# Both MLP entries: the residual sum kept in its PSUM bank, and the norm's matmuls placed behind the first two products

## The chip, the cores and the metric

The kernel runs on one core of a Trainium2 chip. The core has five engines with queues of their own: TensorE (PE in the profile, its weight loads PEld), VectorE (DVE), ScalarE (ACT), GpSimd (POOL) and SyncE (SP), which issues the DMAs here. TensorE writes only to PSUM, which has eight banks of 128 partitions x 512 f32 values. The other working memory is SBUF. The metric is the device time of one execution in microseconds; smaller is better.

## The reference

The model has two residual layers over 512 positions of width 1024, each a mixer followed by an MLP, each behind an RMSNorm. What matters here is the seam between mixer and MLP:

```python
for layer in range(DEPTH):                      # DEPTH = 2
    h = _rmsnorm(x, mix_norm_g[layer])
    x = x + mixer(h) @ w_out                    # layer 0: gMLP + stick-breaking attention
                                                # layer 1: mLSTM
    h = _rmsnorm(x, mlp_norm_g[layer])
    x = x + jnp.square(jax.nn.relu(h @ w1)) @ w2    # w1: 1024 x 4096, w2: 4096 x 1024

def _rmsnorm(x, g):
    ms = jnp.mean(xf * xf, axis=-1, keepdims=True)
    return xf * lax.rsqrt(ms + EPS) * g
```

All of it is f32.

## The kernel before, in words

The residual x lies in SBUF transposed, as `xs`: eight pieces d = 0 to 7 of 128 features x 512 positions. To come close to f32 results, every operand of a product is split into two halves of a shorter type: a high half made by ScalarE (`act.activation(..., Copy)`, L189, L282, L286) and a low half, the rest, made by VectorE (L190, L283, L287; for a few weights by GpSimd). A product is then three matmuls (`mm3`, L290 to L292).

**Weights.** They come as a stream of 128 x 1024 blocks. `w_load` (L182) has SP issue the DMA, `w_split` makes the halves, and `w_take` asks for some blocks and has six more prepared ahead. Five pairs of halves fit in SBUF at once, so a block's halves are made when an older pair has been used up.

**The mixer's output product.** `w_out` (L321 to L328) makes the eight pieces of `mixer(h) @ w_out` one after another. Each takes a PSUM bank from a tag (A has 2 banks, B 3, C 2, O 1), runs its matmuls, and VectorE adds bank and residual into `xs` (L327). In layer 0 a piece is 12 matmuls on banks in the order A, A, B, B; in layer 1 the last part is 6 matmuls a piece on A, A, O.

**The entry.** `enter` (L330 to L342) consumes these pieces. For each it makes the halves of x times the norm's gain, `xhi` and `xlo` (L333), and the square of x on ScalarE (L335, L338); GpSimd adds the squares to one sum `ssq` (L339), VectorE the last of them. The squares share one buffer (tag jk), so a square waits until the one before it is added. When all eight are in, `norm_cols` (L261 to L271) sums `ssq` over the features with four matmuls against a column of 1/1024 (L266, eight instructions in the trace) into a bank of tag C, VectorE adds EPS (L268), and GpSimd raises it to the power -1/2 (L270). `norm_row` (L273 to L279) spreads the result to all partitions with four transposes (L277), and ScalarE copies them out of the bank into `rrow` (L278).

The norm's row scale isn't in `xhi` and `xlo`: it is applied behind the first product of the MLP.

**The MLP.** `mlp` (L620 to L740) runs four groups. In a group, eight first products (24 matmuls each: 8 pieces of x, three matmuls a piece) go to banks of tag A and C in turn; VectorE makes `max(b, 0) * rrow` (L733) and ScalarE squares it (L734). The second products follow, in a Strassen-like scheme (L658 to L714) on banks of tags B and O.

**What sets the order.** The program is written as one stream; the framework notes which instruction needs which, and a planner then orders each engine's queue by a model of the instructions' times, the earlier of two ready ones in the program first. Tiles of one tag take their buffers in program order. Each queue on the chip runs strictly in the order that the planner wrote. The framework puts the accesses of different engines to one bank in order.

Of the kernel before, what the change touches and what calls it, by code (L numbers as in the profile page):

```python
# [132 lines left out]
def _program(ctx, tc, nc, I, O):  # L133
    pool = lambda n, b=1: ctx.enter_context(tc.tile_pool(name=n, bufs=b))
    act, dve, pe, gp = nc.scalar, nc.vector, nc.tensor, nc.gpsimd
    f = lambda t: t.bitcast(F32)
# [121 lines left out]
    onesd = const.tile([P, P], F32, name="onesd")  # L258
    gp.memset(onesd, 1.0 / D)

    def norm_cols(ssq):  # L261

        n = len(ssq)
        b = bank("C")
        for t in range(n):
            pe.matmul(b[:, t:t + 1], lhsT=ssq[t], rhs=onesd[:, 0:1], start=True, stop=True)  # L266
        me = sm(n, f"me{n}")
        dve.tensor_scalar(me, b[:, :n], EPS, None, op0=ALU.add)  # L268
        r = sm(n, f"rc{n}")
        gp.tensor_tensor(r, me, nhalf[:, :n], op=ALU.pow)  # L270
        return me, r  # L271

    def norm_row(r, dst):  # L273

        b = bank("B")
        for t in range(NT):
            pe.transpose(b[:, tts(t)], r[:, t:t + 1].to_broadcast([P, P]), ident)  # L277
        act.activation(dst, b, AF.Copy)  # L278
        rb[0] = dst  # L279

    def split_scaled(dhi, dlo, src, g):
        act.activation(dhi, src, AF.Copy, scale=g)  # L282
        dve.scalar_tensor_tensor(dlo, src, g, f(dhi), op0=ALU.mult, op1=ALU.subtract)  # L283
# [5 lines left out]
    def mm3(out, lh, ll, rh, rl, first, last):  # L289
        pe.matmul(out, lhsT=lh, rhs=rh, start=first, stop=False)  # L290
        pe.matmul(out, lhsT=lh, rhs=rl, start=False, stop=False)  # L291
        pe.matmul(out, lhsT=ll, rhs=rh, start=False, stop=last)  # L292

    junk = pool("junk")
    nhalf = const.tile([P, 8], F32, name="nhalf")
# [12 lines left out]
    tags = itertools.cycle("AAO")  # L308
# [9 lines left out]
                    kt == 0, kt == KT - 1)  # L318
            evac(t, b[:, :width])

    def w_out(hus, ys, tags="A"):  # L321

        for d in range(KT):
            b = bank(tags[d % len(tags)])
            for k, (hi, lo) in enumerate(hus):
                mm3(b, hi[:, tts(d)], lo[:, tts(d)], ys[k][0], ys[k][1], k == 0, k == len(hus) - 1)
            dve.tensor_tensor(xs[:, d, :], b, xs[:, d, :], op=ALU.add)  # L327
            yield d  # L328

    def enter(gen, norm, ssq):  # L330

        for i, d in enumerate(gen):
            split_scaled(xhi[:, d, :], xlo[:, d, :], xs[:, d, :], pc(f"g{norm}", d))  # L333
            if i == 0:
                act.activation(ssq, xs[:, d, :], AF.Square)  # L335
            else:
                j = junk.tile([P, T], F32, name=f"sq{norm}_{d}", tag="jk", bufs=1)
                act.activation(j, xs[:, d, :], AF.Square)  # L338
                (dve if i == KT - 1 else gp).tensor_tensor(ssq, ssq, j, op=ALU.add)  # L339
        r = norm_cols([ssq[:, tts(t)] for t in range(NT)])[1]  # L340
        r1[:] = [r[:, t:t + 1] for t in range(NT)]
        return r  # L342


    ev = ExitStack()
# [4 lines left out]
    with ExitStack() as gx:  # L350
# [22 lines left out]
        b = bank("C")  # L373
# [75 lines left out]
    with ExitStack() as ax:  # L449
        ap = ax.enter_context(tc.tile_pool(name="at", bufs=1))  # L450
# [3 lines left out]
        yb = lambda k, n: (vc[:, :, 2 * k - n].rearrange("p t e d -> p t (e d)") if n <= k else  # L454
                           xlo[:, KT - 1, :].rearrange("p (t c) -> p t c", t=NT))
# [144 lines left out]
        fill.clear()  # L600
        for _ in pieces:
            pass
        ssq = ap.tile([P, T], F32, name="ssq0", tag="m3", bufs=1)
        r = enter(w_out(w_take(4), [(yb(k, 0), yb(k, 1)) for k in range(4)], "AABB"), 1, ssq)
    ev.close()
    nrm = pool("nrm")
    ssq = nrm.tile([P, T], F32, name="ssq")
    rrow = nrm.tile([P, T], F32, name="rrow")
    norm_row(r, rrow)

# [6 lines left out]
    PROD = ("a11", "s2", "n3", "a12", "-a22", "n1", "n4")  # L617
    H = T // 2

    def mlp(last, nxt):  # L620
        with tc.tile_pool(name="mlp", bufs=1) as mp:
            qpool[0] = mp
            accm = mp.tile([P, 4, H], F32, name="accm")
# [34 lines left out]
            def second(g, ops):  # L658

                for s in range(2):  # L660
# [48 lines left out]
                    for e, d in enumerate((4 + 2 * s, 5 + 2 * s)):  # L709
                        add(xs[:, d, :H], b[:, e])  # L710
                        if last and done:
                            nc.sync.dma_start(out=O["out"][d][:, :H], in_=xs[:, d, :H])
                        if done:
                            yield d  # L714

            def out(nb, s):
                for d in (4 * nb + 2 * s, 4 * nb + 2 * s + 1):
                    yield d

            for g in range(NG):  # L720
                ops = {n: [mp.tile([P, 4, H], F32R, name=f"{n}{e}_{g}", tag=f"{n}{e}", bufs=1) for e in "hl"] for n in PROD}
                for q in range(2):
                    hr = []
                    for kb in range(2):
                        hr.append(mp.tile([P, 2, T], F32, name=f"h{g}{q}{kb}", tag="h", bufs=3))
                        for e in range(2):
                            (wh, wl), = w_take(1)
                            b = bank("AC"[e])
                            for kt in range(KT):
                                cs = slice(kt * P, (kt + 1) * P)  # L730
                                mm3(b, wh[:, cs], wl[:, cs], xhi[:, kt, :], xlo[:, kt, :], kt == 0, kt == KT - 1)
                            r = mp.tile([P, T], F32, name=f"r{cnt[0]}", tag="r", bufs=2)
                            dve.scalar_tensor_tensor(r, b, 0.0, rb[0], op0=ALU.max, op1=ALU.mult)  # L733
                            act.activation(hr[kb][:, e, :], r, AF.Square)  # L734
                    operands(q, hr, ops)
                if g == NG - 1 and nxt:
                    norm_row(enter(second(g, ops), nxt, ssq), rrow)
                else:
                    for _ in second(g, ops):
                        pass  # L740

    mlp(False, 2)
# [20 lines left out]
    with ExitStack() as ox:  # L763
# [153 lines left out]
        for op, h, n in ODD:  # L917
# [15 lines left out]
    norm_row(r, rrow)  # L933
    vx.close()
    mlp(True, None)


# [9 lines left out]
```

## Time and profile before

| what | value |
|---|---|
| median of the runs | 1131.99 us |
| profiled execution | 1132.91 us |
| its span, first to last instruction | 1131.1 us |
| TensorE busy | 1107.5 us (98%) |
| VectorE busy | 820.4 us (73%) |
| ScalarE busy | 524.6 us (46%) |
| GpSimd busy | 158.4 us (14%) |
| mean granted TensorE clock | 0.994 |

The profile's lines name an operation by source line, engine and tiles: `L283 DVE ... xlo<-xres,par,xhi` is line 283 of the kernel, on VectorE, which reads `xres` (the residual `xs`), `par` (the gains) and `xhi`, and writes `xlo`. Names that begin with `ps` are PSUM banks by tag. In a timeline a row has start, duration, engine, line, operation and count, and in brackets the idle time of the engine ahead of it with what ended it. Matmul rows overlap, since they are pipelined: what counts is the distance between their starts.

### The profile page before, as it was taken

The numbers are of one execution on the slowest core, as the hardware profiler recorded it, in microseconds if no ns is written. First come the engines' busy times: TensorE is split into PE (matmuls) and PEld (weight loads), VectorE is DVE, ScalarE is ACT, GpSimd is POOL, SyncE is SP. The second block draws the span as 40 slices with busy tenths as digits, with TensorE's granted clock in tenths as the row PEclk, the third lists the DMA queues.
The fourth block names the chain that finished last, engine by engine and source line by source line (L and its number), as shares of the span: only waits on it lengthen the run. The fifth ranks groups of instructions, "written<-read, shape, count | busy, mean of one in ns | idle before, by whom it ended". The sixth has DMA issues, their size and how long they took to land.

```text
span 1131.1 us, 15892 instructions
## 1 busy us (share of the span) xinstructions
PE 1107.5 (98%) x6372; PEld 960.1 (85%) x6372; DVE 820.4 (73%) x1151; ACT 524.6 (46%) x800; POOL 158.4 (14%) x154
## 2 busy tenths in 40 slices
PE   8999999999999999999999999999999999999998
PEld 5788777878988988988988888887899899899898
DVE  7754498468947958858978676679877677677676
ACT  5443687445335335345464543435444444444442
POOL 6316553530000000000230010002100000000000
PEclk8999999999999999999999999999999999999999
DMA  7322310261341331331042303314224224224121
GB/s 231 94 76 87 99 39 1 75 205 57 114 129 56 115 128 56 119 125 57 21 131 75 94 20 112 101 44 149 99 75 149 75 75 149 75 75 150 38 85 66
DMA packets 34506, 105.18 MB, mean 93 GB/s; under 512 B 3712, under 2 KB 10112, under 8 KB 34432
## 3 DMA queue, kind: packets, MB, share of 16 engines
q1 hardware_dynamic: 34432, 104.17, 28.8%
q8 instruction: 50, 0.82, 0.3%
q14 instruction: 24, 0.20, 0.1%
HBM read 102.06 MB, written 2.10 MB: 92 GB/s over the span
## 4 chain that ended last, share of the span: by engine, by line
PE 82%; DVE 8%; POOL 2%; ACT 2%; DMA 2%; issue 2%; SPq 0%; DVEq 0%; POOLq 0%; ACTq 0%
PE psA L292 10%; PE psA L290 10%; PE psA L291 10%; PE psB L674 7%; PE psB L676 7%; PE psB L675 7%; PE psC L292 5%; PE psC L291 5%; PE psC L290 5%; PE psO L290 2%; DVE wl L190 2%; PE psO L291 2%; PE psO L292 2%; DMA wr<-wall 1%; PE psO L676 1%
## 5 line engine op out<-in xcount | busy, mean ns | idle before, releaser
L189 ACT ACTIVATE wh<-wr 128x1024 fp32r<-128x1024 f32 (+1 forms) x124 | 131.2, 1060 | 172.0 <-DMA wr<-wall 65.9
L190 DVE TENSOR_TENSOR wl<-wr,wh 128x1024 fp32r<-128x1024 f32 (+1 forms) x108 | 136.1, 1267 | 81.5 <-ACT wh L189 49.8
L189 ACT ACTIVATE wh<-wq_s 128x1024 fp32r<-128x1024 f32 x64 | 67.0, 1060 | 129.4 <-PE psC L291 57.3
L291 PE MATMUL psA<-xlo,wh 128*128 128x512 f32 x292 | 115.3, 395 | 0.0
L292 PE MATMUL psA<-xhi,wl 128*128 128x512 f32 x288 | 114.2, 396 | 0.5 <-DVE wl L190 0.5
L290 PE MATMUL psA<-xhi,wh 128*128 128x512 f32 x288 | 112.5, 392 | 1.1 <-DVE xres L327 1.1
L292 PE MATMUL psC<-xhi,wl 128*128 128x512 f32 x256 | 102.2, 399 | 0.0
L291 PE MATMUL psC<-xlo,wh 128*128 128x512 f32 x256 | 101.9, 398 | 0.0
L290 PE MATMUL psC<-xhi,wh 128*128 128x512 f32 x256 | 101.0, 394 | 0.0
L290 PE MATMUL psA<-wh,xhi 128*128 128x512 f32 (+2 forms) x232 | 88.5, 384 | 2.6 <-ACT wh L189 2.5
L291 PE MATMUL psA<-wl,xhi 128*128 128x512 f32 (+2 forms) x232 | 88.5, 383 | 1.1 <-DVE wl L190 1.1
L292 PE MATMUL psA<-wh,xlo 128*128 128x512 f32 (+2 forms) x232 | 87.9, 381 | 1.0 <-DVE xlo L287 0.7
L189 ACT ACTIVATE wh<-wq 128x1024 fp32r<-128x1024 f32 x48 | 50.8, 1059 | 79.9 <-PE psB L675 30.2
L339 POOL TENSOR_TENSOR ssq<-ssq,sq 128x512 f32<-128x512 f32 x18 | 31.5, 1751 | 350.5 <-ACT sq L338 350.5
L190 DVE TENSOR_TENSOR wl<-wq_s,wh 128x1024 fp32r<-128x1024 f32 x64 | 77.7, 1222 | 2.5 <-ACT wh L189 2.5
L290 PEld LDWEIGHTS psA<-xhi,wh 128*128 128x128 f32 x288 | 54.7, 190 | 13.9 <-ACT sq L338 1.5
L686 DVE TENSOR_TENSOR xres<-xres,psB 128x512 f32<-128x512 f32 (+1 forms) x96 | 54.9, 594 | 15.4 <-PE psB L676 15.2
L733 DVE SCALAR_TENSOR_TENSOR r<-psC,rrow 128x512 f32<-128x512 f32 x32 | 22.1, 691 | 60.5 <-PE psC L292 60.5
L291 PEld LDWEIGHTS psA<-xlo,wh 128*128 128x128 f32 x292 | 54.9, 188 | 12.3
L292 PEld LDWEIGHTS psA<-xhi,wl 128*128 128x128 f32 x288 | 54.1, 188 | 12.2 <-DVE wl L190 0.8
L190 DVE TENSOR_TENSOR wl<-wq,wh 128x1024 fp32r<-128x1024 f32 x48 | 58.7, 1224 | 2.3 <-ACT wh L189 2.3
L290 PEld LDWEIGHTS psC<-xhi,wh 128*128 128x128 f32 x256 | 49.0, 192 | 11.1
(396 smaller groups left out, 3132.8 us busy)
## 6 DMA issues: line engine op xcount, KB each, us to landing
wr<-wall SPq DMA_DIRECT2D x122, 512.0 KB, 3.6
wq<-wall SPq DMA_DIRECT2D x64, 512.0 KB, 3.7
out<-xres SPq DMA_DIRECT2D x16, 128.0 KB, 1.8
wr<-wv SPq DMA_DIRECT2D x2, 528.0 KB, 3.6
xres<-xT SPq DMA_DIRECT2D x4, 256.0 KB, 7.3
xres<-xT SPq DMA_DIRECT2D x2, 512.0 KB, 9.2
lngb<-lngb SPq DMA_DIRECT2D x1, 512.0 KB, 5.3
sgr<-sgw SPq DMA_DIRECT2D x1, 512.0 KB, 6.1
```

What stands on the lines that cost most here:

```text
L189: act.activation(hi[:, :n], raw, AF.Copy)
L190: (gp if i in POOL_LO else dve).tensor_tensor(lo[:, :n], raw, f(hi[:, :n]), op=ALU.subtract)
L290: pe.matmul(out, lhsT=lh, rhs=rh, start=first, stop=False)
L291: pe.matmul(out, lhsT=lh, rhs=rl, start=False, stop=False)
L292: pe.matmul(out, lhsT=ll, rhs=rh, start=False, stop=last)
L339: (dve if i == KT - 1 else gp).tensor_tensor(ssq, ssq, j, op=ALU.add)
L674: pe.matmul(o, lhsT=lh, rhs=rh, start=first, stop=False, skip_group_check=True)
L675: pe.matmul(o, lhsT=lh, rhs=rl, start=False, stop=False, skip_group_check=True)
L676: pe.matmul(o, lhsT=ll, rhs=rh, start=False, stop=fin, skip_group_check=True)
L686: add = lambda dst, b, op=ALU.add: dve.tensor_tensor(dst, dst, b, op=op)
L733: dve.scalar_tensor_tensor(r, b, 0.0, rb[0], op0=ALU.max, op1=ALU.mult)
```

## The change

There are five edits.

1. `w_out` gets a mode `stay`, used at the two MLP entries: VectorE writes bank + residual back into the bank instead of `xs`, and hands the bank on.
2. `enter` makes `xhi`, `xlo` and the square from that bank, and at the end ScalarE copies the bank to `xs`. The norm is no longer part of `enter`; `norm_of` does it.
3. At both MLPs the norm's matmuls (now in a bank of tag B) are issued behind the last matmul of the first product, and the four transposes behind that of the second. `tc.issue_after(i)` means that TensorE's instructions in the block don't stand ahead of `i` in its queue; they may stand later. The first product's evacuation (L733, L734) waits in a list until the transposes are traced.
4. `norm_row` copies the row scale with VectorE instead of ScalarE. This holds for all three places, that behind the first MLP too.
5. In layer 1 the last part of the output product uses banks A, A, B, B instead of A, A, O. `rrow` and `ssq` are allocated before layer 0's mixer.

The entry of the odd layer (behind the first MLP) keeps its way through `xs` and a norm in tag C.

```diff
-    def norm_cols(ssq):
+    def norm_cols(ssq, tag="C"):
         n = len(ssq)
-        b = bank("C")
+        b = bank(tag)
...
     def norm_row(r, dst):
...
-        act.activation(dst, b, AF.Copy)
+        dve.tensor_copy(dst, b)
...
     def mm3(out, lh, ll, rh, rl, first, last):
...
-        pe.matmul(out, lhsT=ll, rhs=rh, start=False, stop=last)
+        return pe.matmul(out, lhsT=ll, rhs=rh, start=False, stop=last)
...
-    def w_out(hus, ys, tags="A"):
+    def w_out(hus, ys, tags="A", stay=False):
...
-            dve.tensor_tensor(xs[:, d, :], b, xs[:, d, :], op=ALU.add)
-            yield d
+            if stay:
+                dve.tensor_tensor(b, b, xs[:, d, :], op=ALU.add)
+                yield d, b
+            else:
+                dve.tensor_tensor(xs[:, d, :], b, xs[:, d, :], op=ALU.add)
+                yield d, None
     def enter(gen, norm, ssq):
-        for i, d in enumerate(gen):
-            split_scaled(xhi[:, d, :], xlo[:, d, :], xs[:, d, :], pc(f"g{norm}", d))
+        for i, (d, b) in enumerate(gen):
+            src = xs[:, d, :] if b is None else b
+            split_scaled(xhi[:, d, :], xlo[:, d, :], src, pc(f"g{norm}", d))
             if i == 0:
-                act.activation(ssq, xs[:, d, :], AF.Square)
+                act.activation(ssq, src, AF.Square)
             else:
                 j = junk.tile([P, T], F32, name=f"sq{norm}_{d}", tag="jk", bufs=1)
-                act.activation(j, xs[:, d, :], AF.Square)
+                act.activation(j, src, AF.Square)
                 (dve if i == KT - 1 else gp).tensor_tensor(ssq, ssq, j, op=ALU.add)
-        r = norm_cols([ssq[:, tts(t)] for t in range(NT)])[1]
+            if b is not None:
+                act.activation(xs[:, d, :], b, AF.Copy)
+
+    def norm_of(ssq, tag="C"):
+        r = norm_cols([ssq[:, tts(t)] for t in range(NT)], tag)[1]
         r1[:] = [r[:, t:t + 1] for t in range(NT)]
         return r
+
+    def norm_behind(ssq):
+        def behind(e):
+            if e == 0:
+                rb[0] = norm_of(ssq, "B")
+            else:
+                norm_row(rb[0], rrow)
+        return behind
...
-        r = enter(w_out(w_take(4), [(yb(k, 0), yb(k, 1)) for k in range(4)], "AABB"), 1, ssq)
+        enter(w_out(w_take(4), [(yb(k, 0), yb(k, 1)) for k in range(4)], "AABB", True), 1, ssq)
...
-                                mm3(b, wh[:, cs], wl[:, cs], xhi[:, kt, :], xlo[:, kt, :], kt == 0, kt == KT - 1)
-                            r = mp.tile([P, T], F32, name=f"r{cnt[0]}", tag="r", bufs=2)
-                            dve.scalar_tensor_tensor(r, b, 0.0, rb[0], op0=ALU.max, op1=ALU.mult)
-                            act.activation(hr[kb][:, e, :], r, AF.Square)
+                                i = mm3(b, wh[:, cs], wl[:, cs], xhi[:, kt, :], xlo[:, kt, :], kt == 0, kt == KT - 1)
+                            made.append((b, hr[kb][:, e, :]))
+                            if g == q == kb == 0:
+                                with tc.issue_after(i.ins):
+                                    behind(e)
+                                if e == 0:
+                                    continue
+                            while made:
+                                b, h = made.pop(0)
+                                r = mp.tile([P, T], F32, name=f"r{cnt[0]}", tag="r", bufs=2)
+                                dve.scalar_tensor_tensor(r, b, 0.0, rb[0], op0=ALU.max, op1=ALU.mult)
+                                act.activation(h, r, AF.Square)
...
-        r = enter(w_out(w_take(2), y_of(3), "AAO"), 3, ssq)
+        enter(w_out(w_take(2), y_of(3), "AABB", True), 3, ssq)
```

More of the change, by code (lines that the diff above doesn't have):

```diff
@@ L326, in w_out @@
                 mm3(b, hi[:, tts(d)], lo[:, tts(d)], ys[k][0], ys[k][1], k == 0, k == len(hus) - 1)
-            dve.tensor_tensor(xs[:, d, :], b, xs[:, d, :], op=ALU.add)
-            yield d
+            if stay:
[4 more added lines that the diff above has]
+                yield d, None
     def enter(gen, norm, ssq):
-        for i, d in enumerate(gen):
-            split_scaled(xhi[:, d, :], xlo[:, d, :], xs[:, d, :], pc(f"g{norm}", d))
+        for i, (d, b) in enumerate(gen):
+            src = xs[:, d, :] if b is None else b
+            split_scaled(xhi[:, d, :], xlo[:, d, :], src, pc(f"g{norm}", d))
             if i == 0:
-                act.activation(ssq, xs[:, d, :], AF.Square)
+                act.activation(ssq, src, AF.Square)
             else:
                 j = junk.tile([P, T], F32, name=f"sq{norm}_{d}", tag="jk", bufs=1)
-                act.activation(j, xs[:, d, :], AF.Square)
+                act.activation(j, src, AF.Square)
                 (dve if i == KT - 1 else gp).tensor_tensor(ssq, ssq, j, op=ALU.add)
-        r = norm_cols([ssq[:, tts(t)] for t in range(NT)])[1]
+            if b is not None:
+                act.activation(xs[:, d, :], b, AF.Copy)
+    def norm_of(ssq, tag="C"):
+        r = norm_cols([ssq[:, tts(t)] for t in range(NT)], tag)[1]
         r1[:] = [r[:, t:t + 1] for t in range(NT)]
         return r
+    def norm_behind(ssq):
[5 more added lines that the diff above has]
+        return behind
+    nrm = pool("nrm")
+    rrow = nrm.tile([P, T], F32, name="rrow")
+    ssq = nrm.tile([P, T], F32, name="ssq")
     ev = ExitStack()
@@ L602, in _program, with mlp @@
             pass
-        ssq = ap.tile([P, T], F32, name="ssq0", tag="m3", bufs=1)
-        r = enter(w_out(w_take(4), [(yb(k, 0), yb(k, 1)) for k in range(4)], "AABB"), 1, ssq)
+        enter(w_out(w_take(4), [(yb(k, 0), yb(k, 1)) for k in range(4)], "AABB", True), 1, ssq)
     ev.close()
[L606 to L609, printed above, removed]
     PROD = ("a11", "s2", "n3", "a12", "-a22", "n1", "n4")
     H = T // 2
-    def mlp(last, nxt):
+    def mlp(last, nxt, behind):
         with tc.tile_pool(name="mlp", bufs=1) as mp:
@@ L713, in second @@
                         if done:
-                            yield d
+                            yield d, None
             def out(nb, s):
                 for d in (4 * nb + 2 * s, 4 * nb + 2 * s + 1):
-                    yield d
+                    yield d, None
+            made = []
             for g in range(NG):
@@ L730, in mlp @@
                                 cs = slice(kt * P, (kt + 1) * P)
-                                mm3(b, wh[:, cs], wl[:, cs], xhi[:, kt, :], xlo[:, kt, :], kt == 0, kt == KT - 1)
-                            r = mp.tile([P, T], F32, name=f"r{cnt[0]}", tag="r", bufs=2)
-                            dve.scalar_tensor_tensor(r, b, 0.0, rb[0], op0=ALU.max, op1=ALU.mult)
-                            act.activation(hr[kb][:, e, :], r, AF.Square)
+                                i = mm3(b, wh[:, cs], wl[:, cs], xhi[:, kt, :], xlo[:, kt, :], kt == 0, kt == KT - 1)
[10 more added lines that the diff above has]
+                                act.activation(h, r, AF.Square)
                     operands(q, hr, ops)
                 if g == NG - 1 and nxt:
-                    norm_row(enter(second(g, ops), nxt, ssq), rrow)
+                    enter(second(g, ops), nxt, ssq)
+                    norm_row(norm_of(ssq), rrow)
                 else:
@@ L740, in mlp @@
                         pass
-    mlp(False, 2)
+    mlp(False, 2, norm_behind(ssq))
     vx = ExitStack()
@@ L930, in _program @@
                     pass
-        r = enter(w_out(w_take(2), y_of(3), "AAO"), 3, ssq)
+        enter(w_out(w_take(2), y_of(3), "AABB", True), 3, ssq)
         o3.close()
-    norm_row(r, rrow)
     vx.close()
-    mlp(True, None)
+    mlp(True, None, norm_behind(ssq))
 def kernel(**inputs):
```

## The prediction

> **What bounds the kernel now.** I read the page first: engine totals, the chain that ended last, by engine.
>
> ```profile
> span 1131.1 us, 15892 instructions
> PE 1107.5 (98%) x6372; PEld 960.1 (85%) x6372; DVE 820.4 (73%) x1151; ACT 524.6 (46%) x800; POOL 158.4 (14%) x154
> PE 82%; DVE 8%; POOL 2%; ACT 2%; DMA 2%; issue 2%; SPq 0%; DVEq 0%; POOLq 0%; ACTq 0%
> ```
>
> TensorE is busy 1107.5 of 1131.1 us, so all of its idle time is 23.6 us, and no change that leaves the products alone can win more. The change touches two stretches, the entry of the first MLP (about 216 to 254 us) and of the second (about 774 to 810). In the chain in order of time (start, us, what) it leaves TensorE at the first entry:
>
> ```profile
> 235.38 0.64 ACT sq L338
> 236.02 0.07 issue
> 236.09 1.74 POOL ssq L339
> 237.83 0.02 issue
> 237.85 0.64 ACT sq L338
> 238.49 0.02 issue
> 238.51 0.70 DVE ssq L339
> ```
>
> The sum of squares alternates square (ScalarE) and add (GpSimd, the last one VectorE), because one buffer holds the square: 2.47 us from one square to the next here (235.38 to 237.85), and the norm's matmuls wait for the last add. Now TensorE's timeline (start, us, instruction), first entry and then second:
>
> ```profile
> 229.88 0.40 PE L290 MATMUL psA<-xhi,wh 128*128 128x512 f32 x1
> 230.74 0.51 PE L292 MATMUL psA<-xhi,wl 128*128 128x512 f32 x1 [0.46 <-DVE wl L190]
> ...
> 237.33 0.40 PE L291 MATMUL psA<-xlo,wh 128*128 128x512 f32 x1
> 237.56 0.40 PE L292 MATMUL psA<-xhi,wl 128*128 128x512 f32 x1
> 239.35 1.02 PE L266 MATMUL psC<-onesd,ssq 128*128 128x1 f32 x8 [1.39 <-DVE ssq L339]
> ```
>
> ```profile
> 782.92 0.39 PE L292 MATMUL psA<-yoh,wl 128*128 128x512 f32 x1
> 783.48 0.50 PE L290 MATMUL psA<-yoh,wh 128*128 128x512 f32 x1 [0.16 <-DVE xres L327]
> ...
> 784.76 0.39 PE L292 MATMUL psA<-yoh,wl 128*128 128x512 f32 x1
> 786.25 0.47 PE L290 MATMUL psA<-xhi,wh 128*128 128x512 f32 x1 [1.11 <-DVE xres L327]
> ...
> 797.27 0.40 PE L292 MATMUL psA<-xhi,wl 128*128 128x512 f32 x1
> 797.75 1.05 PE L266 MATMUL psC<-onesd,ssq 128*128 128x1 f32 x8
> ```
>
> Matmuls of one stream start 0.23 us apart (237.33 to 237.56). Starts further apart than that are lost time: in the first entry 0.86 - 0.23 = 0.63 us for a weight's low half and 1.79 - 0.23 = 1.56 us for the sum of squares; in the second 0.33 and 1.26 us for a bank that VectorE's add had not left, and 0.25 us for the sum. There is one more loss, in the windows (busy us of TensorE, its weight loads, VectorE, ScalarE, GpSimd, then the granted clock):
>
> ```profile
> 237.80:241.20 3.40, 2.02 (x13) 1.75 (x13) 1.99 (x3) 2.42 (x3) 0.78 (x2) 1.00 0.39 145
> 241.00:245.00 4.00, 4.00 (x12) 3.14 (x11) 1.23 (x1) 0.42 (x1) 1.37 (x2) 0.57 0.88 294
> 568.00:571.40 3.40, 1.77 (x15) 1.56 (x14) 3.40 (x5) 2.21 (x4) 0.17 (x1) 1.00 0.26 67
> ```
>
> The granted clock falls to a mean of 0.57 for 4 us right after the wait for the norm: (1 - 0.57) x 4 = 1.72 us. In the stretch before, 1.02 of the 2.02 us busy is the norm's eight one-column matmuls. A stretch at 568 us with a 1.63 us hole but wide matmuls kept its clock.
>
> **The change, part by part.**
>
> *The norm's matmuls behind the first two products.* Today both products of bank tag A run, then the norm (tag C), then the tag C products: the norm holds up TensorE and the second product stands behind it. With the norm in tag B, four products (each 24 matmuls x 0.23 = 5.6 us) can run on banks A, C, A, C before one needs a bank that only the row scale can free. So the norm's wait (1.56 and 0.25) and the clock fall that follows it (1.72) go, if the planner puts the norm's matmuls late enough: the edit only forbids an earlier place than behind product one. The norm's 1.02 us of matmuls and its four transposes stay on TensorE. The weight wait (0.63) goes too, I think: the second product now has the weight that GpSimd has split, and the third asks 5.6 us later. First entry: 0.63 + 1.56 + 1.72 = 3.91 us to win. Second: 0.25.
>
> *The sum stays in its bank.* The price rows: VectorE, ScalarE and TensorE at the first entry; then the row scale's copy and the split's low half from SBUF and from a bank (ns min/median/max):
>
> ```profile
> 216.73 1.29 DVE L327 TENSOR_TENSOR xres<-psA,xres 128x512 f32<-128x512 f32 x2 [9.55 <-PE psA L292]
> 217.93 1.88 DVE L327 TENSOR_TENSOR xres<-psB,xres 128x512 f32<-128x512 f32 x3
> 219.73 2.44 DVE L283 SCALAR_TENSOR_TENSOR xlo<-xres,par,xhi 128x512 fp32r<-128x512 f32 x2
> 217.45 0.73 ACT L282 ACTIVATE xhi<-xres,par 128x512 fp32r<-128x512 f32 x1 [5.43 <-DVE xres L327]
> 218.09 0.62 ACT L335 ACTIVATE ssq<-xres 128x512 f32<-128x512 f32 x1
> 217.47 0.50 PE L290 MATMUL psA<-vc,wh 128*128 128x512 f32 x1
> L278 ACT ACTIVATE rrow<-psB x3: 598/600/604, 249.0 to 805.8; 128x512 f32<-128x512 f32 x3
> L283 DVE SCALAR_TENSOR_TENSOR xlo<-xres,par,xhi x24: 736/748/2900, 219.7 to 792.9; 128x512 fp32r<-128x512 f32 x24
> L283 DVE SCALAR_TENSOR_TENSOR kl<-psB,kng,kh x8: 727/746/752, 111.6 to 182.2; 128x512 fp32r<-128x512 f32 x8
> ```
>
> What it gives: the low half read from a bank has never taken over 0.75 us, from SBUF up to 2.90, at its worst where GpSimd adds beside it. That is 2 to 4 us less VectorE work an entry, and it removes the second entry's 0.33 and 1.26, where VectorE was late with an add. [...]
>
> What it costs: eight more ScalarE copies an entry, 8 x 0.60 = 4.8 us (row evacuation). ScalarE is 46% busy, and that hides the work, but not the wait that it makes. Today a bank is free as soon as its add ends: piece 4's first matmul starts 217.47, 0.74 us after piece 0's add began. Now the bank is held through add, high half, low half, square and copy. Five pieces close together at 216.7 us there (adds of 0.6 us back to back), and TensorE has nothing but piece 4 to run. Best case: add from 216.73, high half from 217.45, square, copy, paced as today (0.64 + 0.51 + 0.60) ends at 219.2: 1.7 us later than 217.47. Worst: VectorE makes all five adds first as today, the low half runs 219.73 to 220.48, and square and copy (0.62 + 0.60) behind it end at 221.7: 4.2 us. Middle: low half behind two adds, 218.2 to 218.95, then square and copy to 220.3: 2.8 us. I take 2.8, because the high half ends (218.18) about when the second add does. Where a square waits for the square buffer, the next pieces' high halves, the copies and the weights' high halves (L189) queue behind it on ScalarE, and the following banks come free later; pieces 5 and 7 ask 2.8 us (12 matmuls) after each other, more than the 2.47 us of a square's step, so they should not stand. An add written to a bank instead of SBUF has no row: between 0.60 (today's pitch) and 0.69 (its whole length), and I take no difference.
>
> In the second entry a piece is 6 matmuls, 1.4 us, and four to five banks (AABB, three of tag B) instead of three give TensorE pieces 2, 3 and 6 to run while piece 0's bank is held for about 3.5 us: no loss at piece 4. What can come late is the first product's bank, piece 4's, since its square now stands behind three GpSimd adds. Squares of pieces 1 and 4, and the quickest step of an add:
>
> ```profile
> 780.28 0.62 ACT L338 ACTIVATE sq<-xres 128x512 f32<-128x512 f32 x1
> ...
> 788.03 0.62 ACT L338 ACTIVATE sq<-xres 128x512 f32<-128x512 f32 x1
> 783.02 1.28 POOL L339 TENSOR_TENSOR ssq<-ssq,sq 128x512 f32<-128x512 f32 x1 [0.74 <-ACT sq L338]
> ```
>
> Today piece 4's square ends at 788.65, 2.4 us after the first product began (786.25), and nobody cares. With every step at the quick pace (1.28 + 0.74 = 2.02) it ends at 780.90 + 6.06 = 786.96, and TensorE, without its holes of 0.33 and 1.26, is there at 784.66: 2.3 us early. It need not stand, because the second product (tag C, free) can run first; I charge a quarter, 0.6 us, for a planner that turns back to the first product too soon.
>
> *Row scale copied by VectorE.* 0.60 us leaves ScalarE, some 0.69 us (an add's length, 1.29 - 0.60) joins VectorE, three times. Four products cover it at the MLPs; in the odd layer it leaves ScalarE's chain to the gates, where TensorE waits little. I count 0, between -0.5 and +0.7. The pools that now open earlier issue nothing, and no DMA moves past SP's queue by the edit.
>
> **Sum.** First entry: -3.91 + 2.8 = -1.1. Second: -0.25 - 0.33 - 1.26 + 0.6 = -1.2. Together -2.3 on the profiled execution: its 1132.91 us (span 1131.1 and 1.8 around it) becomes 1130.6. The median of the runs, 1131.99, is 0.9 below that execution, so I forecast 1129.7.
>
> **Rivals.**
>
> *The banks' hold wins.* Its place is piece 4 of the first entry: the hole there is 4.2 us instead of 2.8, and the gate takes it badly. The stretch 237.8 to 241.2 had about 1.0 us of wide matmuls and lost its clock, the one at 568 us had 1.77 and kept it, so a hole of 4.2 us lowers the clock for some 4 us: 1.72 us. Sum of that entry -3.91 + 4.2 + 1.72 = +2.0; the second, where the planner puts the first product first, -1.84 + 2.3 = +0.5. The time would be 1131.99 + 2.5 = 1134.5. With the second entry's 1.2 us won it decides from a hole of 3.91 + 1.2 = 5.1 us on, or 3.4 us if the clock falls too. For it: today's VectorE order (five adds before a low half). Against: that order was laid out for banks that the add frees. [...]
>
> *All is won.* The planner lets the square and copy go at once and interleaves pieces so that piece 4 hardly waits: -3.91 - 1.84 = -5.75, time 1126.2. Against it: at 217 us TensorE has no other piece with a bank.
>
> *The norm still waits.* The planner orders engines by modelled times. If it thinks the sum of squares is ready when product one ends (about 226 + 2.8 + 5.6 = 234.4), while the chip has it near 238, TensorE stands 3.6 us and the clock falls again: then the change doesn't do what it says. First entry -0.63 + 2.8 + (3.6 - 1.56) = +4.2, second -1.2: 1135.0. For it: at the first entry the chip did come later than TensorE did. Against: with products to fill in, only an early estimate puts it there.
>
> **How the numbers follow.** Forecast 0.50 (1128 to 1131.5), banks' hold 0.22, all won 0.12, norm waits 0.10; 0.06 for a plan that shifts elsewhere, by up to some 30 us either way. The range 1126.0 to 1135.2 reaches from the case where all is won to the two slower ones. Two per cent is 22.6 us, about what a measurement of this kernel tells from no change; TensorE's whole idle time barely reaches it, so faster by that much 0.01, within 0.97, slower 0.02.
>
> **What would show it.** Right: no wait of L266 on the sum; the granted clock at 1.00 behind the first entry's products; low halves from a bank at 0.75 us; a new hole of 1.7 to 4.2 us ahead of piece 4, released by ScalarE. Wrong: a fall of the clock in that hole, the norm's matmuls waiting as before, or the first product waiting over a microsecond for a square.

## The result, and the profile after

The changed kernel takes 1143.69 us (median of 6 runs, 1142.43 to 1145.72), the kernel before 1132.89 us beside it: a ratio of 1.0095 with a 95% interval from 1.0080 to 1.0111. That is under the 2% of the prediction's classes, but it is slower, by 10.8 us, where a gain of 2.3 us was forecast, and it lies outside the range. One of the six runs of the kernel before took 1893.9 us; without it the median of the others is 1131.99 us, and the loss 11.7 us. The profiled execution took 1143.89 us. First the page of after: span and engines.

```profile
span 1142.1 us, 15919 instructions
PE 1110.1 (97%) x6372; PEld 964.0 (84%) x6372; DVE 815.5 (71%) x1154; ACT 529.8 (46%) x813; POOL 157.4 (14%) x154
```

The totals hardly move, and VectorE is even 4.9 us less busy. The time was lost in waits and in the clock. In the line numbers of after, L329 is the add into the bank, L341 and L344 the squares, L345 the sum of squares, L347 the copy from the bank to `xs`, L760 the former L733.

**First entry.** The timeline of after (start, duration, engine, line, tiles; in brackets the idle time ahead and its releaser):

```profile
217.58 1.30 DVE L329 TENSOR_TENSOR psA<-psA,xres 128x512 f32<-128x512 f32 x2 [9.55 <-PE psA L292]
218.31 1.28 ACT L282 ACTIVATE xhi<-psA,par 128x512 fp32r<-128x512 f32 x2 [5.42 <-DVE psA L329]
218.78 1.89 DVE L329 TENSOR_TENSOR psB<-psB,xres 128x512 f32<-128x512 f32 x3
219.51 1.88 ACT L282 ACTIVATE xhi<-psB,par 128x512 fp32r<-128x512 f32 x3
220.70 1.41 DVE L283 SCALAR_TENSOR_TENSOR xlo<-psA,par,xhi 128x512 fp32r<-128x512 f32 x2
221.49 0.60 ACT L341 ACTIVATE ssq<-psA 128x512 f32<-128x512 f32 x1
221.98 0.59 ACT L347 ACTIVATE xres<-psA 128x512 f32<-128x512 f32 x1
...
222.62 0.80 PE L290 MATMUL psA<-vc,wh 128*128 128x512 f32 x1 [4.17 <-ACT xres L347]
...
245.52 0.95 PE L266 MATMUL psB<-onesd,ssq 128*128 128x1 f32 x8
```

VectorE makes all five adds (217.58 to 220.67) before the first low half, ScalarE all five high halves before the first square. So piece 0's bank is held until 222.57, and piece 4 starts 4.17 us later than TensorE could. By distance of starts the hole is 4.32 us. The norm's matmuls, at 245.52, wait for nothing.

**Second entry.** The timeline of after around its pieces, and then around its norm:

```profile
779.80 1.29 DVE L329 TENSOR_TENSOR psB<-psB,xres 128x512 f32<-128x512 f32 x2
...
781.87 0.40 PE L292 MATMUL psA<-yoh,wl 128*128 128x512 f32 x1
...
782.74 0.69 DVE L329 TENSOR_TENSOR psA<-psA,xres 128x512 f32<-128x512 f32 x1
...
783.46 0.69 ACT L282 ACTIVATE xhi<-psA,par 128x512 fp32r<-128x512 f32 x1
784.20 0.49 PE L290 MATMUL psC<-xhi,wh 128*128 128x512 f32 x1 [1.93 <-ACT xhi L282]
...
785.91 1.40 DVE L283 SCALAR_TENSOR_TENSOR xlo<-psA,par,xhi 128x512 fp32r<-128x512 f32 x2
...
786.70 0.50 PE L291 MATMUL psC<-xlo,wh 128*128 128x512 f32 x1 [2.01 <-DVE xlo L283]
787.17 0.59 ACT L347 ACTIVATE xres<-psA 128x512 f32<-128x512 f32 x1
...
790.91 0.40 PE L290 MATMUL psA<-yoh,wh 128*128 128x512 f32 x1
```

```profile
809.18 0.95 PE L266 MATMUL psB<-onesd,ssq 128*128 128x1 f32 x8
...
810.45 1.93 POOL L270 TENSOR_TENSOR rc<-me,nhalf 128x4 f32<-128x4 f32 x1 [6.51 <-DVE me L268]
...
816.13 0.60 PE L277 MATMUL psB<-ident,rc 128*128 128x128 f32 x4
...
817.40 0.68 DVE L278 COPY rrow<-psB 128x512 f32<-128x512 f32 x1
819.13 0.68 DVE L760 SCALAR_TENSOR_TENSOR r<-psA,rrow 128x512 f32<-128x512 f32 x1
...
819.87 0.50 PE L290 MATMUL psA<-xhi,wh 128*128 128x512 f32 x1 [2.90 <-DVE r L760]
```

The planner has pieces 2, 3 and 6 (tag B) run ahead of pieces 0 and 1 (tag A), whose last matmul is at 781.87: VectorE adds into banks of tag B from 779.80 on, into the first of tag A only at 782.74. Then both A banks have to be evacuated, and TensorE's queue has twelve matmuls of the second product (tag C) next. They stand for the high half (a hole of 2.10 us by starts) and for the low half (2.27 us), and pieces 4, 5 and 7 are queued behind them: they run from 790.91 on, although piece 4's bank was free at 787.76. Later the row scale is late: the root is ready at 812.38, the transposes stand at 816.13, 3.75 us behind it, their copy and the first L760 wait in VectorE's queue, and the fifth product starts with a hole of 3.15 us.

**The clock.** The windows of after behind these holes (busy us of TensorE, its loads, VectorE, ScalarE, GpSimd; then the granted clock):

```profile
222.60:227.00 4.40, 4.38 (x10) 3.52 (x11) 1.49 (x3) 2.61 (x6) 2.55 (x2) 0.50 0.00 0
...
786.80:790.60 3.80, 3.80 (x10) 3.02 (x11) 0.51 (x1) 2.91 (x6) 1.56 (x2) 0.55 0.00 0
...
821.20:824.70 3.50, 3.50 (x10) 2.73 (x9) 3.50 (x7) 3.50 (x7) 0.00 (x0) 0.51 0.00 0
```

Lost are about 0.50 x 4.4 = 2.2, 0.45 x 3.8 = 1.7 and 0.49 x 3.5 = 1.7 us. First entry of after: 4.32 + 2.2 = 6.5 us lost, where 3.91 were lost before: +2.6. Second: 2.10 + 2.27 + 0.54 (a weight's low half at 797 us) + 3.15 + 1.7 + 1.7 = 11.5, where 1.84 were lost: +9.6. Together that is +12.2, and the span grew by 11.0. Where the rest is shows when TensorE's matmuls are counted and those of the same number are compared in the two profiles: after is 0.85 us late already when the first entry begins, 3.4 us late behind it (256 us of before), only 1.9 us late when the second begins (776 us), 11.3 us late behind that (830 us), and 11.0 at the end. So the entries cost 2.5 and 9.4 us, and 1.5 us were won between them; what won these stays open.

### The profile page after: what moved, and what is told of

The parts are those of the page before. It is cut to its first block, busy times and chain, and to the rows that moved or that the text cites. A ratio compares the mean times of both kernels' runs of the same rounds, so it can differ in the third digit from the quotient of the medians.

```text
span 1142.1 us, 15919 instructions
## 1 busy us (share of the span) xinstructions
PE 1110.1 (97%) x6372; PEld 964.0 (84%) x6372; DVE 815.5 (71%) x1154; ACT 529.8 (46%) x813; POOL 157.4 (14%) x154
## 4 chain that ended last, share of the span: by engine, by line
PE 87%; DVE 6%; issue 2%; POOL 2%; DMA 2%; ACT 1%; SPq 0%; DVEq 0%; POOLq 0%; ACTq 0%
PE psA L290 11%; PE psA L292 11%; PE psA L291 11%; PE psB L692 7%; PE psB L694 7%; PE psB L693 7%; PE psC L292 5%; PE psC L291 5%; PE psC L290 5%; PE psO L290 2%; PE psO L291 2%; PE psO L292 2%; DVE wl L190 1%; PE psO L694 1%; PE psO L692 1%
## 5 line engine op out<-in xcount | busy, mean ns | idle before, releaser
L345 POOL TENSOR_TENSOR ssq<-ssq,sq 128x512 f32<-128x512 f32 x18 | 29.0, 1610 | 356.7 <-ACT sq L344 356.7
L291 PEld LDWEIGHTS psA<-xlo,wh 128*128 128x128 f32 x292 | 55.5, 190 | 12.2
L760 DVE SCALAR_TENSOR_TENSOR r<-psC,rrow 128x512 f32<-128x512 f32 x32 | 22.1, 690 | 60.3 <-PE psC L292 60.3
L291 PEld LDWEIGHTS psC<-xlo,wh 128*128 128x128 f32 x256 | 48.6, 190 | 13.8 <-DVE xlo L283 2.6
```

## The experiments

The theory from the two profiles is this: the bank's hold costs the time, at both entries ("hold"). The rival: it is the norm that the edit binds behind the products ("norm"). The first four kernels take the change apart; in the diffs the lines removed are those of the changed kernel, unless another is named. Each kernel was measured beside the kernel before, whose median was 1132.9 to 1134.1 us in the four sittings; a difference between two kernels of different sittings carries that spread.

**The norm moved, no bank held.**

```diff
-        enter(w_out(..., "AABB", True), 1, ssq)
+        enter(w_out(..., "AABB"), 1, ssq)
-        enter(w_out(w_take(2), y_of(3), "AABB", True), 3, ssq)
+        enter(w_out(w_take(2), y_of(3), "AAO"), 3, ssq)
```

> The changed kernel with the sum going to the residual in SBUF as before at both entries (layer 1's last part on A, A, O again); the norm in tag B behind the first two products and VectorE's copy of the row scale stay. Theory 'hold' (the held banks are the loss, at both entries): the holes of 4.3 us ahead of piece 4 and of 2.1 + 2.3 us in the second entry are gone with their falls of the clock; at the first entry the 1.56 us wait and the fall of the clock behind it (1.7 us) are gone too. What stays is a late row scale at the fourth product's end, 2 to 3 us an entry, because the planner puts the transposes almost at the end of the fourth product. Sum about -1 to +2 us against the kernel before, ratio 0.999 to 1.002. Rival 'norm' (the binding behind product one makes the row scale late and that is the loss): +5 us or more, 1.005 and above.

Measured: 1133.54 us beside 1133.17, ratio 1.0007 [0.9993, 1.0021]. The timeline at the first entry:

```profile
250.12 0.60 PE L277 MATMUL psB<-ident,rc 128*128 128x128 f32 x4
251.46 0.68 DVE L278 COPY rrow<-psB 128x512 f32<-128x512 f32 x1
253.20 0.68 DVE L760 SCALAR_TENSOR_TENSOR r<-psA,rrow 128x512 f32<-128x512 f32 x1
...
254.02 0.47 PE L290 MATMUL psA<-xhi,wh 128*128 128x512 f32 x1 [3.30 <-DVE r L760]
```

The wait for the norm and its fall of the clock are gone (the clock is 1.00 from 239.0 to 243.0 us), as is the weight's wait. In their place TensorE waits 3.34 us (by starts) for the row scale, because the planner put the transposes behind the whole of the fourth product; at the second entry it is 2.59 us. The move alone wins nothing, and costs nothing.

**The banks held, the norm where it was.**

```diff
-    mlp(False, 2, norm_behind(ssq))
+    norm_row(norm_of(ssq), rrow)
+    mlp(False, 2, None)
```

(the same at the second MLP; the row scale copied by ScalarE again)

> The changed kernel with the norm as before (tag C, ahead of the products) and the row scale copied by ScalarE: only the sum that stays in its bank is left of the change (with A, A, B, B in layer 1). Theory 'hold': first entry +4.3 us hole and some 2 us of slow clock, less up to 3.3 us of the old wait and its clock; second entry: the planner has no tag C product to put ahead of pieces 4 to 7, so one hole of 3 to 5 us ahead of piece 4 with a fall of the clock of 1.7. Sum +5 to +9 us, ratio 1.005 to 1.008. Rival 'norm': about none, 0.998 to 1.002.

Measured: 1144.21 us, ratio 1.0100 [1.0087, 1.0112]: the whole loss, and more than the 5 to 9 us of the theory. The timeline at the second entry:

```profile
786.60 0.80 PE L290 MATMUL psA<-yoh,wh 128*128 128x512 f32 x1 [5.56 <-ACT xres L347]
...
796.02 0.51 PE L290 MATMUL psA<-xhi,wh 128*128 128x512 f32 x1 [2.70 <-ACT xres L347]
```

Here nothing of the second product stands ahead, and piece 4 waits for its bank in one hole of 5.72 us. Then the first product waits 2.86 us more, until ScalarE's copy has left the bank of piece 4, whose square and copy stood behind two weights' high halves in ScalarE's queue (792.42 to 794.42). The hole of the first entry is 4.32 us as in after. "Norm" falls.

**The bank held at one entry only.** Two kernels, each with `True` left out at the other entry.

```diff
-        enter(w_out(w_take(2), y_of(3), "AABB", True), 3, ssq)
+        enter(w_out(w_take(2), y_of(3), "AAO"), 3, ssq)
```

> The changed kernel with the bank kept at the first entry alone; second entry through the residual on A, A, O, norm behind products at both. Theory 'hold', from the two profiles: first entry +2.5 us as in the changed kernel, second entry +1 to +2 for a late row scale: +2 to +5 us, ratio 1.002 to 1.004. If the loss of the second entry came from the norm's place and not from the bank, it would be near the changed kernel's +10.8 us, 1.009.

> The changed kernel with the bank kept at the second entry alone; first entry through the residual. Theory 'hold': first entry -1 to -2 us (wait and clock gone, late row scale 2 us), second entry +8.7 us as in the changed kernel: +5 to +8 us, ratio 1.005 to 1.007. This and the run with the first entry alone should add up to the changed kernel's +10.8 plus the run with neither; if they do not, the planner's reshuffling is the cause rather than the two places.

Measured: first entry alone 1136.03 us, 1.0028 [1.0017, 1.0039]; second alone 1142.33 us, 1.0088 [1.0073, 1.0102]. That is +2.9 and +9.2 us over before's 1133.17. Both contain the moved norm (+0.4), so the sum is 2.9 + 9.2 - 0.4 = 11.7, and the changed kernel has 10.8. The two places add up, within the noise, and the second is three times the first. The second alone lies above its expected 5 to 8 us.

**What the clock costs in the first hole.** Fourteen matmuls that serve nothing fill it.

```diff
             if b is not None:
                 act.activation(xs[:, d, :], b, AF.Copy)
+            if norm == 1 and i == 3:
+                o = bank("O")
+                for _ in range(14):
+                    pe.matmul(o, lhsT=xhi[:, 0, :P], rhs=xhi[:, 0, :], start=True, stop=True)
```

> The changed kernel (median 1143.7 beside 1132.9 of before) with 14 matmuls more, whose result nobody reads, behind piece 3 of the first entry: they read the high half of piece 0 and write the bank of tag O, and end about when piece 4's bank is handed over. The hole of 4.3 us is filled with work that serves nothing, so that only the clock differs. Theory 'the gap itself lowers the clock': no half clock at 221 us, piece 4's matmuls 0.23 us apart instead of 0.43, about 2 us less than the changed kernel, 1141.7. Rival 'the hole is the whole price, the clock falls anyway or costs nothing': 1143.7 as before, half clock still there at about 221 us.

Measured: 1142.52 us, 1.0082 [1.0063, 1.0101]. The window behind the filled hole:

```profile
222.70:226.70 4.00, 4.00 (x19) 3.23 (x18) 1.53 (x3) 2.63 (x5) 2.12 (x2) 1.00 0.00 0
```

19 matmuls at a clock of 1.00 where after has 10 at 0.50: here it was the gap that lowered the clock, not the hold. In time the two can't be told apart surely (-1.2 us, with intervals that overlap), also since 0.99 us of the gain came back as a hole ahead of the fifth product, where the row scale is now late here as well.

**VectorE's order in the first entry.**

```diff
             if stay:
-                dve.tensor_tensor(b, b, xs[:, d, :], op=ALU.add)
+                with (tc.issue_after(los[d - 2].ins) if d > 1 and len(hus) == 4 else ExitStack()):
+                    dve.tensor_tensor(b, b, xs[:, d, :], op=ALU.add)
```

(`los` lists the low halves' instructions)

> The changed kernel with one order more at the first entry: VectorE's add of piece d does not stand ahead of the low half of piece d-2, so that VectorE makes two adds, then the low half of piece 0, and so on, instead of five adds first. Theory 'VectorE's order sizes the hole': the middle case of the prediction, 2.8 us ahead of piece 4 instead of 4.3, released by ScalarE's copy; time 1.5 us less than the changed kernel, 1142.2, and 1140.2 if the clock then stays up. Rival 'the bank's hold by itself sizes it, in any order': the hole stays above 4 us and the time at 1143.7.

Measured: 1143.19 us, 1.0085 [1.0067, 1.0103]. The timeline:

```profile
219.02 1.30 DVE L332 TENSOR_TENSOR psA<-psA,xres 128x512 f32<-128x512 f32 x2 [9.55 <-PE psA L292]
...
220.47 0.75 DVE L283 SCALAR_TENSOR_TENSOR xlo<-psA,par,xhi 128x512 fp32r<-128x512 f32 x1 [0.16 <-ACT xhi L282]
...
221.26 0.60 ACT L344 ACTIVATE ssq<-psA 128x512 f32<-128x512 f32 x1 [0.22 <-DVE xlo L283]
...
221.75 0.59 ACT L350 ACTIVATE xres<-psA 128x512 f32<-128x512 f32 x1
...
222.40 0.50 PE L290 MATMUL psA<-vc,wh 128*128 128x512 f32 x1 [2.50 <-ACT xres L350]
```

The hole is 2.65 us by starts, where the prediction's middle case had 2.8: VectorE's order sizes it, and add, high half, low half, square and copy take their turns on the bank (ScalarE waits 0.22 us for VectorE's low half). The time doesn't show it: in the profile the stretch from the hole to the fifth product is 37.2 us for after's 38.7, the runs differ by 0.5 us with overlapping intervals. The two profiles can't be compared by their spans: the profiled execution of this kernel reaches the entry 1.4 us later than that of after, before the edit has any effect. Even this order leaves a hole, a fall of the clock (a mean of 0.61 from 222.7 to 226.7 us, where after has 0.50) and 0.70 us ahead of the fifth product.

**The row scale bound.** The last nine matmuls of the fourth product stand behind the transposes (`row[0]` is the last of them).

```diff
-                                i = mm3(b, ...)
+                                with (tc.issue_after(row[0].ins) if g == q == 0 and kb == e == 1 and kt >= 5 else ExitStack()):
+                                    i = mm3(b, ...)
```

> The changed kernel, with the last nine matmuls of the fourth product of both MLPs bound behind the four transposes of the row scale, so that the planner cannot put these late. Theory 'the second entry has two losses, the banks' hold (2.1 + 2.3 us and a clock fall) and a row scale that comes late (3.2 us and a clock fall of 1.7)': the second one goes to under 1 us, the first one stays; 1143.7 - 4 = 1139.7. Rival 'one loss, in which the late start of the first product decides and the row scale only follows it': TensorE waits at the transposes instead, for the sum of squares or its root, and the time stays within 1 us of 1143.7.

Measured: 1139.77 us, 1.0062 [1.0044, 1.0081], as the theory had it. The timeline and the window at the second entry (L764 is the former L760):

```profile
814.27 0.60 PE L277 MATMUL psB<-ident,rc 128*128 128x128 f32 x4
...
817.39 0.50 PE L291 MATMUL psA<-xhi,wh 128*128 128x512 f32 x1 [0.42 <-DVE r L764]
```

```profile
817.30:821.00 3.70, 3.61 (x16) 3.00 (x17) 3.70 (x7) 3.49 (x7) 0.00 (x0) 1.00 0.45 142
```

The hole of 3.15 us is 0.59 us, and the clock stays up: the late row scale was 3.9 us of the second entry's loss, apart from the hold.

**TensorE's order in the second entry.** Pieces 2 and 3 behind piece 1.

```diff
-            for k, (hi, lo) in enumerate(hus):
-                mm3(b, ...)
+            with (tc.issue_after(lastmm.ins) if stay and len(hus) == 2 and d in (2, 3) else ExitStack()):
+                for k, (hi, lo) in enumerate(hus):
+                    i = mm3(b, ...)
+            if d < 2:
+                lastmm = i
```

> The changed kernel with TensorE's order bound at the second entry: pieces 2 and 3 (banks of tag B) of the output product stand behind piece 1 (tag A), where the planner had put pieces 2, 3 and 6 ahead of pieces 0 and 1. Theory 'the second entry lost its cover by this order: both A banks were filled last, so nothing was left to run while they were evacuated': pieces 2, 3 and 6 (4.2 us of matmuls) now cover the hold of pieces 0 and 1, the holes of 2.1 and 2.3 us in front of the second product shrink to 1.5 us or less together, and the late row scale (3.2 us) stays: 1143.7 - 3.5 = 1140.2. Rival 'the second entry is bound by VectorE and ScalarE, which are late in any order': the holes move to another piece and stay at 3 us or more, 1142.5 to 1144.

Measured: 1137.97 us, 1.0041 [1.0028, 1.0054], 5.7 us less than the changed kernel, and 2.2 less than the theory's 1140.2, which didn't count the fall of the clock. The timeline:

```profile
777.82 1.29 DVE L332 TENSOR_TENSOR psA<-psA,xres 128x512 f32<-128x512 f32 x2
...
781.06 0.59 ACT L350 ACTIVATE xres<-psA 128x512 f32<-128x512 f32 x1
...
781.57 0.40 PE L292 MATMUL psB<-yoh,wl 128*128 128x512 f32 x1
...
781.81 0.39 PE L290 MATMUL psC<-xhi,wh 128*128 128x512 f32 x1
```

From the last of pieces 2, 3 and 6 to the second product there are 0.24 us, no wait; the holes of 2.10 and 2.27 us and their fall of the clock are gone (1.00 from 781.8 to 785.8 us), though piece 0's bank is still held for 3.8 us (777.82 to 781.65; in after 5.0, 782.74 to 787.76). The 3.15 us for the row scale stay. So at the second entry the hold was not the cause by itself: the planner's order had used up its cover.

**A shorter hold.** ScalarE copies the bank first and squares the copy.

```diff
+            if b is not None:
+                act.activation(xs[:, d, :], b, AF.Copy)
+                src = xs[:, d, :]
             if i == 0:
                 act.activation(ssq, src, AF.Square)
...
-            if b is not None:
-                act.activation(xs[:, d, :], b, AF.Copy)
```

> The changed kernel in which ScalarE copies the bank to SBUF ahead of the square, and squares the copy: a bank is held for the add, the high half, the low half and the copy, no longer for the square, whose buffer waits for GpSimd's sum. Theory 'the hold is the row of evacuations taken in turns behind VectorE's low half': one step of 0.5 us is saved, the first entry's hole is 3.8 us instead of 4.3, the second entry loses as before, 1142.5 to 1143.5. Rival 'the square's buffer and GpSimd's chain of sums hold the banks': both entries gain, the second most, to 1140 or less.

Measured: 1141.99 us, 1.0070 [1.0048, 1.0091]. The timeline at the first entry:

```profile
221.35 0.79 PE L290 MATMUL psA<-vc,wh 128*128 128x512 f32 x1 [3.67 <-ACT xres L341]
```

The hole is 3.83 us by starts: one step less, as expected. In the second entry the hole of 2.10 us stays; that of 2.27 us becomes 0.33, since the planner now lays pieces between the parts of the second product. The time is half a microsecond under the theory's range, and its interval is too wide to decide between the two by time alone. The hole at the first entry decides for the first entry; for the second the run leaves it open, because the planner's order changed with the edit.

**The row scale's copy by itself.** The kernel before with this one line changed.

```diff
-        act.activation(dst, b, AF.Copy)
+        dve.tensor_copy(dst, b)
```

> The kernel before, with nothing but the row scale copied by VectorE in place of ScalarE, at three places. The prediction counted 0 for it, between -0.5 and +0.7: 1133 beside 1133 of before, ratio 0.9995 to 1.0006. Rival 'VectorE's queue delays the copy': the products behind the norm wait for the row scale, 1134 or more.

Measured: 1134.05 us beside 1134.14, 0.9998 [0.9984, 1.0012]. No loss shows, as the prediction counted; the interval, -1.8 to +1.4 us, is wider than its -0.5 to +0.7.

**Two versions without the hold.** The first is the kernel with the norm moved, sums in SBUF, banks A, A, B, B in the second entry and the transposes bound as above.

> The norm behind the first products and VectorE's copy of the row scale kept, the sums back in SBUF at both entries (no bank is held), the last part of layer 1's output product on banks A, A, B, B, and the transposes bound ahead of the last nine matmuls of the fourth product. Theory 'moving the norm wins once the row scale is in time': the kernel with the norm alone moved had 1133.5 and two holes of 3.3 and 2.6 us ahead of the fifth product; these go to under 1 us, and the second entry's holes of 0.32 and 1.27 of before become smaller with a fourth bank; 1133.5 - 5 = 1128.5, faster than before (1133). Rival 'the chain from the sum of squares to the row scale is too long for four products': a hole of 2 us or more stays ahead of the transposes or the fifth product, and the time is 1132 to 1134.

Measured: 1131.19 us beside 1133.4, 0.9979 [0.9966, 0.9993]. Between theory and rival: of the hole behind the second entry's norm 0.26 us are left, but at the first one TensorE still waits twice, 1.07 and 1.70 us by starts.

```profile
246.84 0.65 PE L277 MATMUL psB<-ident,rc 128*128 128x128 f32 x4 [0.90 <-POOL rc L270]
...
251.10 0.47 PE L291 MATMUL psA<-xhi,wh 128*128 128x512 f32 x1 [1.52 <-DVE r L764]
```

The fourth bank won next to nothing: holes of 0.37 and 1.09 us stay where 0.33 and 1.26 were. The second version gives the fifth product a bank of tag B, which no row scale has to free, and binds the last 18 of that product's 24 matmuls, not the end of the fourth product, behind the transposes (the lines removed are those of the first version):

```diff
-                            b = bank("AC"[e])
+                            fifth = g == kb == e == 0 and q == 1
+                            b = bank("B" if fifth else "AC"[e])
...
-                                with (tc.issue_after(row[0].ins) if g == q == 0 and kb == e == 1 and kt >= 5 else ExitStack()):
+                                with (tc.issue_after(row[0].ins) if fifth and kt >= 2 else ExitStack()):
```

> As the run with the transposes bound and the sums in SBUF (1131.2), but the fifth product takes a bank of tag B in place of tag A, so that five products, not four, can run before TensorE needs a bank that only the row scale frees. Theory 'the row scale's chain is what still stands in front of the fifth product': the hole of 1.7 us there goes, that of 1.1 us in front of the transposes may stay; 1129.5 or less. Rival 'TensorE waits for the chain at the transposes just as long': 1131.

Measured: 1127.51 us (1125.5 to 1128.82) beside 1134.14, ratio 0.9947 [0.9930, 0.9964]: faster than both kernels. Its profiled execution has a span of 1127.0 us. The window that holds the transposes and the start of the fifth product:

```profile
250.00:254.00 4.00, 4.00 (x21) 3.26 (x20) 3.18 (x4) 1.74 (x2) 0.00 (x0) 1.00 0.54 147
```

Neither entry has a hole behind its norm any more, and the clock stays at 1.00. So half of the change, the moved norm, wins 6.6 us beside the kernel before, once it is bound and has five products of cover and not four. Matmul by matmul its profile gains 3.9 us on that of before at the first entry, the 3.91 that the prediction saw there, and 5.3 us from the start of that entry to the end; the rest of the 6.6 between the medians isn't located.

## Why the prediction was wrong

- **"So the norm's wait (1.56 and 0.25) and the clock fall that follows it (1.72) go": right.** L266 waits at neither entry of the changed kernel, and with the norm alone moved no fall of the clock is left at the first entry. That no other fall took its place there is not explained by the hole that the late row scale makes: with the second bank alone held it is as long, 3.36 us for 3.34, and the clock was lost (see the last section). The 0.63 us for the weight's low half went too, and 0.54 us for another one came at the second entry. The rival "the norm still waits" had no place.
- **"I take 2.8" for the hole ahead of piece 4: wrong choice between bounds that held to 0.1 us.** 4.32 us were measured, the worst case (4.2), and by its mechanism: five adds, then the low halves. I chose the middle because a low half could run behind two adds. But the profile of before had shown the order of VectorE's queue, its five adds from 216.73 us on and the first low half at 219.73, and after has the same (217.58 and 220.70). With the middle order imposed the hole is 2.65 us.
- **No fall of the clock in that hole: wrong by 2.2 us.** The forecast's sum had none; the rival "the banks' hold wins" had 4.2 + 1.72 and came near for the first entry (+2.0; +2.6 by the holes and windows of the profile). The hole that I had chosen did not keep the clock either: in the run with the middle order the clock behind its 2.65 us was 0.61 from 222.7 to 226.7 us.
- **"Give TensorE pieces 2, 3 and 6 to run while piece 0's bank is held ...: no loss at piece 4": the step that failed most.** The planner ran those pieces before pieces 0 and 1. The free bank of tag C, on which I counted as a way out ("the second product can run first"), was no cover: its matmuls were taken while their operands were not made, and TensorE waited for these. Where no such product stood ahead, in the kernel with the banks alone held, piece 4 and the first product waited longer, 5.72 and 2.86 us; the second of these is the late bank for which I charged a quarter, 0.6 us. In the changed kernel holes of 4.4 us and 1.7 us of clock stand at pieces 0 to 4; 5.7 us came back with the order alone changed. For the whole second entry I had forecast -1.2 us, and it lost 9.4. The rival's figure for this entry, +0.5, was as wrong.
- **"Four products cover it": false.** The row scale came 2.6 to 3.3 us late at three places (both entries with the norm alone moved, the second of after), because the planner put the transposes at the end of the fourth product, and the copy and L760 stood behind weights' low halves in VectorE's queue. At the first entry of after, where TensorE was late itself, the transposes stand earlier and no hole shows. Priced at 0, it was 3.9 us at the second entry.
- **The price rows held.** Low halves from a bank and adds into one, in the groups of after (ns min/median/max):

```profile
L283 DVE SCALAR_TENSOR_TENSOR xlo<-psA,par,xhi x8: 741/744/751, 220.7 to 797.1; 128x512 fp32r<-128x512 f32 x8
L329 DVE TENSOR_TENSOR psB<-psB,xres x8: 690/691/700, 218.8 to 795.4; 128x512 f32<-128x512 f32 x8
L345 POOL TENSOR_TENSOR ssq<-ssq,sq x18: 1271/1336/4224, 223.1 to 801.8; 128x512 f32<-128x512 f32 x18
```

The low half is at 0.75 us, the add into a bank (0.69 to 0.70 us) about as long as one into SBUF (0.68 in before), and GpSimd's adds of the squares took a median of 1.34 us, 1.60 before; what made them faster no run shows. One reading was off: the low half of 2.90 us (at 225.45 in before) stood beside GpSimd's low half of a weight (224.97, 2.84 us), not beside an add of squares. In the changed kernel all of this was work off the path, and 4.9 us less of VectorE didn't shorten it. Whether it removes the second entry's 0.33 and 1.26 is not shown by itself: they are gone in the kernel with the order bound there and stay where the sums are in SBUF, but these two differ in the order too. The terms of work were right, and the terms of order were wrong: I priced each wait as if the planner would find the order that hides it.

## What to carry to other kernels

Count for how long a bank is held, not only what is done with it, and who is next in the queue of each engine that holds it: a bank that one add used to free was held through five steps on two engines. Where an order is a planner's, price a step at its bad end unless the order is bound, and bind it where it matters: one line each, for two pieces' order and for four transposes, was worth 5.7 and 3.9 us here. When work is moved behind other work, check the chain behind it for the same cover; here the sum was in time and the row scale wasn't.

## What the runs showed of the hardware

Equal holes did not cost the clock the same. The kernel with the norm alone moved and the one with the second bank alone held have the same hole at the first entry, 3.34 and 3.36 us; the second lost its clock. The windows of the first and then of the second, those of the second laid on the time at which its clock fell:

```profile
249.12:252.53 3.41, 1.60 (x10) 1.09 (x8) 2.21 (x3) 2.00 (x2) 0.00 (x0) 1.00 0.37 135
252.53:255.95 3.42, 1.93 (x8) 1.61 (x9) 3.32 (x6) 2.01 (x4) 0.00 (x0) 1.00 0.42 152
```

```profile
249.16:252.57 3.41, 1.43 (x9) 0.96 (x7) 2.36 (x3) 1.96 (x2) 0.00 (x0) 1.00 0.40 139
252.57:255.98 3.41, 2.07 (x5) 1.71 (x6) 3.31 (x6) 2.15 (x4) 0.00 (x0) 0.50 0.40 144
```

In both the hole lies across the two windows. In the first kernel TensorE was busy for 1.60 of the first 3.41 us (0.47), and the clock stayed at 1.00; in the second for 1.43 (0.42), and the clock was 0.50 in the next 3.41 us. (A matmul's end is modelled in the profile, so the shares are rough.) In before, 2.02 us of the 3.41 ahead of its half clock (237.93 to 241.34) were busy, 1.02 of them with the norm's one-column matmuls. There the half clock lasted 3.41 us (241.34 to 244.75); in after it lasted 6.83, 3.41 and 3.41 us (from 220.48, 787.10 and 821.23 on). So the length of a hole did not tell what it would cost: 3.34 us kept the clock, while 3.36 us, 2.65 us (VectorE's order bound) and, in before, 1.56 us lost it. What decides between the two these runs do not show.
